# A sparse-attention and RWKV-7 trunk: another order in its weave, other buffers for rotation and compression, one score pass moved ahead

## The chip, the cores and the metric

The kernel runs on one core of one Trainium2 chip. The time is the device time of one execution in microseconds (us). Five engines take part: PE (TensorE, with its weight loads as PEld), DVE (VectorE), ACT (ScalarE), POOL (GpSimd) and SP (SyncE), which here issues all DMAs, one behind the other.

## The reference

One layer on x of 1024 tokens by 1024 channels, then a final RMSNorm. All arithmetic is float32.

```python
h = rms_norm(x, norm_g)
proj = h @ w_in                      # one projection, its columns for two groups of heads
# group B, 8 heads of 64: RWKV-7, a state per head
state = state * w + (state @ -kk) (kk * a) + v k ;  y = state @ r
# y: normed by group, plus a bonus, times silu(g_rwkv)
# group A, 8 heads of 64 on 2 K/V heads: three attentions
k_cmp, v_cmp = compress_blocks(...)  # 32-token blocks: silu(flat @ w1) @ w2
o_cmp = softmax(q k_cmp) v_cmp ;  top 8 blocks of 64 by its probabilities
q_rot, ks, kw = partial_rope(...)    # 16 of 64 dimensions rotated
o_sel = attention over the 8 chosen blocks ;  o_win = over a window of 512
# gated sum of the three, times silu(g_nsa)
x + concat(A, B) @ w_out
```

## The kernel before, in words

**Filler.** The projection runs as a stream of matmuls of 128 by 512, the filler: for each column group three products (high by high, high by low, low by high, of operands that are split in two parts: `gn2h` and `gn2l` are the two parts of `gn2r`, a weight as it is loaded; `gn` are four groups of the gate of group A, `gr` of the gate of group B). `filler.step(n)` puts n of them into PE's order. A group's weights come in two halves; a half is loaded, ACT copies it to the high part (L342), DVE subtracts for the low one (L344).

**Weave.** The recurrence of group B runs over eight chunks of 128 tokens, one weave each (`weave(n)`, L1242). A weave has 12 steps. A step puts a burst of small matmuls of the chain into PE's order (`pc`, `py`; the chain is what hands the state on from chunk to chunk), then half of its filler quota (7 or 8 matmuls in all), then the side pieces of the step, then the other half. Side pieces prepare the next chunks: elementwise work (`pss`, `pt`, `pbt`, `pn`), products (`pp`), a triangular inverse in 31 steps on POOL (`lt`, `ltmp`, L584 and L586, for which `la` is loaded through DRAM: `la<-dA`), values, and the norm of the chunk before (`nq`, `ny`, `pyn`). From the table in the program each side piece has its step.

**Seam.** In weaves 6 and 7 the buffers of the elementwise work have become free and a pool for group A is opened, with six buffers under the one tag c4. `rotate()` (L755) turns q and the window and selection keys: it loads q and keys twice (`ropa`, and `ropw` with the two halves exchanged), and tables of cosines and sines (`ropc`, `rops`); DVE multiplies `ropa` (L777), POOL `ropw` (L778), DVE adds (L781), ACT copies the sum to its high part `roph`, POOL subtracts for the low one `ropl` (L785), and four stores per set go out. `compress(b)` (L793) loads keys or values (`kc`), their weights w1 in four tiles and w2; DVE and POOL add positions (`xc`, L815), PE multiplies (`pcm`, 16 matmuls for each of the four w1 tiles).

**Prologue.** After the last weave come 12 filler matmuls, the norm of chunk 7, and then, under an order by hand for PE, the first score passes of group A: `row_max` finds the maximum score of each row (PE writes scores to `pd` and `ps`, DVE reduces them to `bm`, L982 and L994), PE turns the result (`pnm`), DVE writes it into q (L1009). `compressed` does the attention over compressed blocks (`pcs`, `pct`, `poc`). Between the pieces stand filler matmuls.

**Stages.** Then follow eight query tiles in the order (1, 5, 4, 3, 6, 2, 7, 0), each in two branches b=0 (chosen blocks) and b=1 (window). A branch computes scores `pst`, exponentials `prob` (ACT), their sums `acc` (POOL) and values `po`, and at its end `pz`, `prt` (which needs POOL's `wide`). Score passes of the next tile are spread over each branch. POOL also multiplies `yr` by the gate `sg` and splits the output weights (`wol`).

**Order.** PE's and POOL's order in the weaves, and PE's alone behind them, is that of the program text. The order of DVE, ACT and SP is set by a scheduler from priorities and its own simulated times. Each engine runs its list strictly in order.

Of the kernel before, what the change touches and what calls it, by code (L numbers as in the profile page):

```python
# [20 lines left out]
S = 1024  # L21
# [53 lines left out]
def trunk_kernel(ctx, tc, x, norm_g, w_in, cmp_pos_k, cmp_w1_k, cmp_w2_k, cmp_pos_v, cmp_w1_v,  # L75
# [666 lines left out]
    def split_out(scale, dfull, dh, dl, rows0):  # L742
# [9 lines left out]
            dma(dl[rows0:rows0 + 128, hs], al)  # L752
        return use

    def rotate():  # L755


        ct, sn = c4([128, S], FT, "ropc"), c4([128, S], FT, "rops")
        sets = []
        for src, dh, dl in ((dQ, dQH, dQL), (dKFa, dKHa, dKLa)):  # L760
            v = src.rearrange("(h d) t -> h d t", d=64)
            n = v.shape[0] * 8
            a, w = c4([128, S], FT, "ropa"), c4([128, S], FT, "ropw")
            if n < 64:
                for t in (a, w):
                    G.memset(t[n:64], 0.0)
            for hf in range(2):
                rows = slice(hf * 64, hf * 64 + n)
                dma(a[rows], v[:, hf * 8:hf * 8 + 8, :])
                dma(w[rows], v[:, 8 - hf * 8:16 - hf * 8, :])  # L770
            sets.append((slice(0, 64 + n), n, a, w, dh, dl))
        for i, tb in enumerate((ct, sn)):
            for hf in range(2):
                dma(tb[hf * 64:hf * 64 + 64], rope[i:i + 1, hf * 8:hf * 8 + 8].to_broadcast([8, 8, S]))
        yield
        for rows, n, a, w, dh, dl in sets:
            V.tensor_tensor(a[rows], a[rows], ct[rows], op=OP.mult)  # L777
            G.tensor_tensor(w[rows], w[rows], sn[rows], op=OP.mult)  # L778
            yield
        for rows, n, a, w, dh, dl in sets:  # L780
            V.tensor_tensor(a[rows], a[rows], w[rows], op=OP.add)  # L781
            h_ = c4([128, S], FR, "roph")
            A.activation(h_[rows], a[rows], AF.Copy)
            l_ = c4([128, S], FR, "ropl")
            G.tensor_tensor(l_[rows], a[rows], h_[rows].bitcast(FT), op=OP.subtract)  # L785
            for d, t in ((dh, h_), (dl, l_)):
                v = d.rearrange("(h d) t -> h d t", d=64)
                for hf in range(2):
                    dma(v[:, hf * 8:hf * 8 + 8, :], t[hf * 64:hf * 64 + n])
            yield  # L790


    def compress(b, w1, w2):  # L793
# [9 lines left out]
        s2 = cp.tile([128, 2, 126], FT, tag="cs2", name="cs2", bufs=1)  # L803

        def load(q):
            wt = c4([128, 4, 256], FT, "w1")
            dma(wt, w1v[:, q * 4:q * 4 + 4, :])
            return wt

# [435 lines left out]
    def weave(n, sides, quota):  # L1245


        chain = wkv_chain(n)
        for j in range(12):
            with tc.high_priority(offset=200000):  # L1250
                next(chain)
            filler.step(quota // 2)
            for gen in sides.get(j, ()):
                piece(gen)
            filler.step(quota - quota // 2)
        whole(chain)

    TRI, EDGE, TRI_T, EDGE_T = range(4)
# [6 lines left out]
    def c4(shape, dt, name):  # L1265
        return cp.tile(shape, dt, tag="c4", name=name, bufs=6)
# [36 lines left out]
    with tc.manual_schedule(engines={E.PE, E.Pool}):  # L1303
        keys = []
        nxt_elem = wkv_load(2) or wkv_elementwise(2)

        def call(f):
            f()
            yield

        for n in range(8):
            sides = {}

            def side(gen, *steps):
                for j in steps:
                    sides.setdefault(j, []).append(gen)

            elem = nxt_elem
            if n < 7:
                side(wkv_values(n + 1), 0, 1)  # L1320
                inv = wkv_inverse(n + 1)
            if n < 6:
                side(elem, *((0, 1, 2, 3, 3, 4, 5, 8) if n == 0 else (0, 1, 2, 3, 4, 5, 8)))
            if 0 < n < 7:
                side(prod, 0, 1, 2, 3, 4, 5)
            if n > 0:
                side(wkv_norm(n - 1), 0, 2, 4)
            if n < 6:
                prod = wkv_products(n + 2)
                side(prod, 6, 7, 7, 10, 11)  # L1330
            if n < 5:
                def ahead(n=n):
                    if n == 1:
                        filler.through("v3")
                    wkv_load(n + 3)
                nxt_elem = wkv_elementwise(n + 3)
                side(call(ahead), 2)
                side(nxt_elem, 11)
            if n < 7:
                side(inv, 9, 10, 11)  # L1340
            if n == 6:
                side(call(open_keys), 1)

                def begin(gen):
                    keys.append(gen)
                    next(gen)

                def nxt(k, *steps):
                    for j in steps:
                        side(call(lambda: next(keys[k])), j)  # L1350

                side(call(lambda: (filler.through("q3"), begin(rotate()))), 1)
                nxt(0, 6, 7, 8, 9)
                side(call(lambda: begin(compress(0, cmp_w1_k, cmp_w2_k))), 9)
            if n == 7:
                nxt(1, 0, 1, 2, 3, 4, 5)
                side(call(lambda: begin(compress(1, cmp_w1_v, cmp_w2_v))), 3)
                nxt(2, 6, 7, 8, 9, 10, 11)
            weave(n, sides, (7, 7, 7, 8, 8, 8, 7, 7)[n])
        for g in keys:  # L1360
            assert next(g, None) is None
        norm = wkv_norm(7)
        next(norm)
        next(norm)
        filler.step(12)
        next(norm)
# [30 lines left out]
    with tc.manual_schedule(engines=PEQ):  # L1397
        L = load_queries(TILES[0], 0)
        dma(keep, late[:, L_IMP:])
        load_keys(0)  # L1400
        load_keys(1)
        L1 = load_queries(TILES[1], 1)
        load_values(0)
        load_values(1)
        comp, rm0, rm1 = compressed(TILES[0], L), row_max(TILES[0], 0, L), row_max(TILES[0], 1, L)
        com1 = compressed(TILES[1], L1)
        filler.step(30)
        for gen, n in ((comp, 10), (rm0, 5), (rm0, 5), (comp, 5), (rm0, 5), (rm0, 5), (comp, 5),
                       (rm1, 5), (com1, 5), (rm1, 5), (rm1, 5), (rm1, 5), (rm0, 8), (com1, 5),
                       (rm1, 5), (com1, 0)):  # L1410
            next(gen)
            filler.step(n)
        for gen in (comp, rm0, rm1, com1):
            assert next(gen, None) is None
        filler.through("gr3")
# [56 lines left out]
    with tc.manual_schedule(engines=PEQ):  # L1472
        for n, i in enumerate(TILES):
# [7 lines left out]
            for b in range(2):  # L1481
# [4 lines left out]
                if b == 0:  # L1486
                    if n:
                        side.add(row_max(i, 1, L), row_max_pieces(i, 1), 0.0, 0.8)
                    if 0 < n < 7:
                        side.add(compressed(j, L1), 3, 0.0, 0.9)  # L1490
                elif n < 7:
                    side.add(row_max(j, 0, L1), row_max_pieces(j, 0), 0.0, 0.8)
                if n == 1:
                    side.add(wout, 4)
# [44 lines left out]
```

## Time and profile before

| what | value |
|---|---|
| three runs | 1043.26 us median (1038.44 to 1045.9) |
| the profiled execution | 1040.26 us, span 1038.5 us |
| PE busy | 930.2 us, 90% of the span, 6353 matmuls |
| DVE, ACT, POOL busy | 584.0, 335.5, 448.2 us |
| granted clock of PE, mean | 0.951 |
| the chain that ended last | PE 60%, DVE 10%, DMA 9%, POOL 7%, SP's issue 6% |

Busy time is what instructions took on an engine; the rest of the span the engine waited or had nothing. The chain is followed back from the last instruction to what released each one. In the trace, weaves 0 to 5 run from 198 to about 480 us, weave 6 from 480.8, weave 7 from 527.6 to about 583; the prologue begins at 594, the stage of the first tile at 650, that of the second at about 676.

### The profile page before, as it was taken

How to read it: one execution, taken by the hardware profiler on the slowest of the kernel's cores; microseconds unless marked ns; L12 is line 12 of the kernel's file. 1: busy time of each engine (PE TensorE's matmuls, PEld its weight loads, DVE VectorE, ACT ScalarE, POOL GpSimd, SP SyncE). 2: the span in 40 equal slices, each digit the busy share in tenths (PEclk: the TensorE clock that was granted, in tenths of full speed). 3: DMA queues.
4: the chain of work that ended last, by engine and by line, in shares of the span. 5: the costliest groups of instructions: out<-in, count | busy, mean ns of one | idle time of the engine just before them, and what ended most of it. 6: DMA issues, size and time to landing. Idle time of an engine off the chain costs nothing.

```text
span 1038.5 us, 17087 instructions
## 1 busy us (share of the span) xinstructions
PE 930.2 (90%) x6353; PEld 658.6 (63%) x6353; DVE 584.0 (56%) x1245; ACT 335.5 (32%) x650; POOL 448.2 (43%) x732
## 2 busy tenths in 40 slices
PE   5999999989998999899669978689999999889976
PEld 4888777766676766677458756354565656455555
DVE  7533545555575657374424335677659856685544
ACT  5533233224233443243121212433333333224321
POOL 3100153466483847444521120577463555246521
PEclk9999999999999999799889988879999999899989
DMA  7433453424426453536476293741132312231121
GB/s 259 125 102 102 125 157 108 130 76 116 135 76 172 134 154 119 131 106 170 116 218 192 65 203 95 212 122 31 41 63 79 77 46 69 53 80 33 39 84 41
DMA packets 154429, 115.66 MB, mean 111 GB/s; under 512 B 54369, under 2 KB 132266, under 8 KB 154346
## 3 DMA queue, kind: packets, MB, share of 16 engines
q1 hardware_dynamic: 154346, 114.57, 40.3%
q8 instruction: 50, 0.82, 0.3%
q14 instruction: 33, 0.27, 0.1%
HBM read 76.19 MB, written 35.19 MB: 107 GB/s over the span
## 4 chain that ended last, share of the span: by engine, by line
PE 60%; DVE 10%; DMA 9%; POOL 7%; SPq 6%; issue 5%; ACT 2%; POOLq 0%; DVEq 0%; ACTq 0%
PE pout L113 7%; SPq L85 6%; PE pst L113 6%; PE po L113 5%; PE p_r L113 4%; PE p_k L113 3%; PE p_gn L113 3%; PE p_gr L113 3%; PE p_q L113 3%; PE pc L113 2%; POOL lt L586 2%; POOL ltmp L584 2%; PE ps L113 2%; PE pd L113 2%; PE pcm L113 2%
## 5 line engine op out<-in xcount | busy, mean ns | idle before, releaser
L584 POOL TENSOR_TENSOR ltmp<-la,lt 128x60 f32<-128x60 f32 (+24 forms) x248 | 83.7, 337 | 65.3 <-DMA la<-dA 42.7
L1042 ACT ACTIVATE prob<-pst 128x512 f32<-128x512 f32 x132 | 74.6, 593 | 109.9 <-PE pst L113 106.3
L1055 POOL TENSOR_TENSOR acc<-acc,prob 128x1024 f32<-128x1024 f32 x36 | 86.7, 2409 | 45.1 <-ACT prob L1042 44.9
L586 POOL TENSOR_TENSOR lt<-lt,ltmp 128x60 f32<-128x60 f32 (+24 forms) x248 | 87.6, 353 | 18.8
L113 PE MATMUL pst<-q,k 128*128 128x512 f32 (+1 forms) x264 | 82.3, 430 | 0.0
L994 DVE TENSOR_REDUCE bm<-ps 128x6 f32<-128x384 f32 (+1 forms) x106 | 63.5, 613 | 26.6 <-PE ps L113 26.0
L113 PE MATMUL po<-prob,vt 128*64 128x512 f32 x264 | 75.1, 648 | 0.0
L1055 POOL TENSOR_TENSOR acc<-prob 128x1024 f32<-128x1024 f32 x14 | 33.7, 2410 | 82.6 <-ACT prob L1042 82.6
L113 PEld LDWEIGHTS pst<-q,k 128*128 128x128 f32 (+1 forms) x264 | 48.9, 196 | 14.9 <-issue 5.7
L113 PE MATMUL pout<-woh,mh 128*128 128x512 f32 x128 | 57.6, 450 | 0.2 <-DVE xt L1153 0.2
L113 PE MATMUL ps<-k,q 128*128 128x384 f32 (+3 forms) x136 | 45.4, 386 | 7.7 <-DVE bm L994 3.7
L113 PE MATMUL pout<-wol,mh 128*128 128x512 f32 x128 | 51.3, 401 | 0.0
L113 PE MATMUL pout<-woh,ml 128*128 128x512 f32 x128 | 51.2, 400 | 0.0
L113 PEld LDWEIGHTS ps<-k,q 128*128 128x128 f32 x136 | 25.6, 205 | 35.2 <-DVE bm L994 14.3
L982 DVE TENSOR_REDUCE bm<-pd 128x8 f32<-128x512 f32 x40 | 27.4, 688 | 26.2 <-PE pd L113 26.0
L113 PEld LDWEIGHTS pout<-woh,mh 128*128 128x128 f32 x128 | 25.1, 196 | 20.7 <-issue 17.8
L683 ACT ACTIVATE x<-pc 64x128 f32<-64x128 f32 x32 | 8.7, 272 | 75.4 <-DVE x L682 75.2
L113 PE MATMUL pd<-k,q 128*128 128x128 f32 x160 | 31.1, 321 | 2.1 <-POOL k L868 2.1
L1077 POOL TENSOR_TENSOR wide<-rr,ones 128x512 f32<-128x512 f32 x16 | 17.1, 1068 | 36.1 <-DVE rr L1073 34.1
L1069 DVE TENSOR_REDUCE zz<-pz 128x4 f32<-128x512 f32 x32 | 21.8, 684 | 13.4 <-PE pz L1067 13.0
L1153 DVE TENSOR_TENSOR xt<-pout,xt 128x512 f32<-128x512 f32 x16 | 11.1, 691 | 32.4 <-PE pout L113 32.4
L113 PEld LDWEIGHTS pd<-k,q 128*128 128x128 f32 x160 | 25.9, 204 | 4.0 <-POOL k L868 2.4
(518 smaller groups left out, 2447.7 us busy)
## 6 DMA issues: line engine op xcount, KB each, us to landing
dM<-mix SPq DMA_DIRECT2D x24, 256.0 KB
q<-dQH SPq DMA_DIRECT2D x22, 256.0 KB
la<-dA SPq DMA_DIRECT2D x32, 128.0 KB
xt<-in_x_dram SPq DMA_DIRECT2D x8, 512.0 KB
out_dram<-xt SPq DMA_DIRECT2D x16, 256.0 KB
x<-in_x_dram SPq DMA_DIRECT2D x7, 512.0 KB
mixk<-dM SPq DMA_DIRECT2D x8, 256.0 KB
mixr<-dM SPq DMA_DIRECT2D x8, 256.0 KB
```

Source lines behind the costliest of these rows:

```text
L85: return nc.sync.dma_start(plain(o), plain(i))
L113: return T.matmul(o, l, r, start=start, stop=stop)
L584: G.tensor_tensor(tv, la[:, j:j + 1, j + 1:].to_broadcast([128, m, n]), lt[:, :m, j:j + 1].to_broadcast([128, m, n]), op=OP.mult)
L586: G.tensor_tensor(lt[:, :m, j + 1:], lt[:, :m, j + 1:], tv, op=OP.add)
L683: gate["A"] = A.activation(x1[1][HP[1], c:8:4, :], pv[HP[1], :, 64:128], AF.Copy)
L982: V.tensor_reduce(bm[:, g * 4:g * 4 + 4, j:j + 2], p.rearrange("p (r b c) -> p r b c", b=2, c=64), axis=AX.X, op=OP.max)
L994: V.tensor_reduce(bm[:, h0:h0 + n, j:j + 2 * w], p[:, :n * w * 128].rearrange("p (h b c) -> p h b c", h=n, c=64), axis=AX.X, op=OP.max)
L1042: A.activation(pr[:, g * 512:(g + 1) * 512], p, AF.Exp)
L1055: G.tensor_tensor(s, self.acc, pr, op=OP.add)
L1069: V.tensor_reduce(zz[:, g, :], p.rearrange("p (r k) -> p r k", r=4), axis=AX.X, op=OP.add)
L1077: G.tensor_tensor(wide, rr.rearrange("p r g -> p (r g)").unsqueeze(2).to_broadcast([128, 8, 64]), ones64.unsqueeze(1).to_broadcast([128, 8 ...
L1153: V.tensor_tensor(xt[:, hs], p, xt[:, hs], op=OP.add)
```

## The change

It has four parts. (a) In a weave the side pieces of a step stand directly behind the burst, and the whole filler quota follows them. (b) The tables of `rotate` lie in two buffers that the RWKV part no longer uses (tags g0, g1), and its split is made in place: ACT copies the sum into `ropw`, POOL subtracts in `ropa`; the four w1 tiles of the first `compress` lie in four such buffers (ar, la, g0, g1). (c) In weave 6 the steps of `rotate` are 7 to 10, where they were 6 to 9; the first `compress` is begun at step 6 and runs at steps 9, 10, 11 of weave 6 and 0, 1, 2 of weave 7, where it was begun at 9 and ran at 0 to 5 of weave 7; the second is begun at step 0 and runs at 4 to 9, where it was 3 and 6 to 11. (d) The score pass of the second tile for b=0 moves from the first stage (its branch b=1) to the end of the prologue, with three filler matmuls behind each of its pieces; the prologue begins with 40 filler matmuls where it had 30, and has fewer between its pieces.

```diff
@@ -752,10 +752,16 @@
             dma(dl[rows0:rows0 + 128, hs], al)
         return use
 
+    def spare(tag):
+
+        if tag == "la":
+            return r2("la", 1, (128, 32, 32)).rearrange("p a b -> p (a b)")
+        return r2(tag, 3, (128, 8, 2, 64)).rearrange("p a b c -> p (a b c)")
+
     def rotate():
 
 
-        ct, sn = c4([128, S], FT, "ropc"), c4([128, S], FT, "rops")
+        ct, sn = (spare(t) for t in ("g0", "g1"))
         sets = []
         for src, dh, dl in ((dQ, dQH, dQL), (dKFa, dKHa, dKLa)):
             v = src.rearrange("(h d) t -> h d t", d=64)
@@ -779,11 +785,9 @@
             yield
         for rows, n, a, w, dh, dl in sets:
             V.tensor_tensor(a[rows], a[rows], w[rows], op=OP.add)
-            h_ = c4([128, S], FR, "roph")
-            A.activation(h_[rows], a[rows], AF.Copy)
-            l_ = c4([128, S], FR, "ropl")
-            G.tensor_tensor(l_[rows], a[rows], h_[rows].bitcast(FT), op=OP.subtract)
-            for d, t in ((dh, h_), (dl, l_)):
+            A.activation(w.bitcast(FR)[rows], a[rows], AF.Copy)
+            G.tensor_tensor(a.bitcast(FR)[rows], a[rows], w[rows], op=OP.subtract)
+            for d, t in ((dh, w.bitcast(FR)), (dl, a.bitcast(FR))):
                 v = d.rearrange("(h d) t -> h d t", d=64)
                 for hf in range(2):
                     dma(v[:, hf * 8:hf * 8 + 8, :], t[hf * 64:hf * 64 + n])
@@ -803,7 +807,8 @@
         s2 = cp.tile([128, 2, 126], FT, tag="cs2", name="cs2", bufs=1)
 
         def load(q):
-            wt = c4([128, 4, 256], FT, "w1")
+            wt = c4([128, 4, 256], FT, "w1") if b else (
+                spare(("ar", "la", "g0", "g1")[q]).rearrange("p (u c) -> p u c", c=256))
             dma(wt, w1v[:, q * 4:q * 4 + 4, :])
             return wt
 
@@ -1249,10 +1254,9 @@
         for j in range(12):
             with tc.high_priority(offset=200000):
                 next(chain)
-            filler.step(quota // 2)
             for gen in sides.get(j, ()):
                 piece(gen)
-            filler.step(quota - quota // 2)
+            filler.step(quota)
         whole(chain)
 
     TRI, EDGE, TRI_T, EDGE_T = range(4)
@@ -1350,12 +1354,13 @@
                         side(call(lambda: next(keys[k])), j)
 
                 side(call(lambda: (filler.through("q3"), begin(rotate()))), 1)
-                nxt(0, 6, 7, 8, 9)
-                side(call(lambda: begin(compress(0, cmp_w1_k, cmp_w2_k))), 9)
+                nxt(0, 7, 8, 9, 10)
+                side(call(lambda: begin(compress(0, cmp_w1_k, cmp_w2_k))), 6)
+                nxt(1, 9, 10, 11)
             if n == 7:
-                nxt(1, 0, 1, 2, 3, 4, 5)
-                side(call(lambda: begin(compress(1, cmp_w1_v, cmp_w2_v))), 3)
-                nxt(2, 6, 7, 8, 9, 10, 11)
+                nxt(1, 0, 1, 2)
+                side(call(lambda: begin(compress(1, cmp_w1_v, cmp_w2_v))), 0)
+                nxt(2, 4, 5, 6, 7, 8, 9)
             weave(n, sides, (7, 7, 7, 8, 8, 8, 7, 7)[n])
         for g in keys:
             assert next(g, None) is None
@@ -1404,12 +1409,15 @@
         load_values(1)
         comp, rm0, rm1 = compressed(TILES[0], L), row_max(TILES[0], 0, L), row_max(TILES[0], 1, L)
         com1 = compressed(TILES[1], L1)
-        filler.step(30)
-        for gen, n in ((comp, 10), (rm0, 5), (rm0, 5), (comp, 5), (rm0, 5), (rm0, 5), (comp, 5),
-                       (rm1, 5), (com1, 5), (rm1, 5), (rm1, 5), (rm1, 5), (rm0, 8), (com1, 5),
-                       (rm1, 5), (com1, 0)):
+        rm2 = row_max(TILES[1], 0, L1)
+        filler.step(40)
+        for gen, n in ((comp, 8), (rm0, 4), (rm0, 4), (comp, 4), (rm0, 3), (rm0, 3), (comp, 3),
+                       (rm1, 3), (com1, 3), (rm1, 3), (rm1, 3), (rm1, 3), (rm0, 4), (com1, 3),
+                       (rm1, 3), (com1, 3)):
             next(gen)
             filler.step(n)
+        for _ in rm2:
+            filler.step(3)
         for gen in (comp, rm0, rm1, com1):
             assert next(gen, None) is None
         filler.through("gr3")
@@ -1488,7 +1496,7 @@
                         side.add(row_max(i, 1, L), row_max_pieces(i, 1), 0.0, 0.8)
                     if 0 < n < 7:
                         side.add(compressed(j, L1), 3, 0.0, 0.9)
-                elif n < 7:
+                elif 0 < n < 7:
                     side.add(row_max(j, 0, L1), row_max_pieces(j, 0), 0.0, 0.8)
                 if n == 1:
                     side.add(wout, 4)
```

PE in weave 3: the last product of a burst (`py`), the side pieces of that step (`pss`, `pt`) and filler (`p_kw`). Before:

```order
L113 MATMUL py<-g_2337,x_2593 64x64
L113 MATMUL p_kw<-hh_109,kwh 128x512
L113 MATMUL p_kw<-hh_109,kwl 128x512
L113 MATMUL p_kw<-hl_111,kwh 128x512
L113 MATMUL pss<-mi,s_3703 128x2 x4
L113 MATMUL pt_3713<-tt,t_3612 32x32 x16
L113 MATMUL p_kw<-hh_109,kwh 128x512
L113 MATMUL p_kw<-hh_109,kwl 128x512
L113 MATMUL p_kw<-hl_111,kwh 128x512
L113 MATMUL p_kw<-hh_109,kwh 128x512
```

The same place now:

```order
L113 MATMUL py<-g_2334,x_2590 64x64
L113 MATMUL pss<-mi,s_3700 128x2 x4
L113 MATMUL pt_3710<-tt,t_3605 32x32 x16
L113 MATMUL p_kw<-hh_109,kwh 128x512
L113 MATMUL p_kw<-hh_109,kwl 128x512
L113 MATMUL p_kw<-hl_111,kwh 128x512
L113 MATMUL p_kw<-hh_109,kwh 128x512
L113 MATMUL p_kw<-hh_109,kwl 128x512
L113 MATMUL p_kw<-hl_111,kwh 128x512
L113 MATMUL p_kw<-hh_109,kwh 128x512
```

Three filler matmuls that stood ahead of the side pieces stand behind them.

SP in weave 6, behind the loads for `rotate` of q and of the keys (`dKFa`). Before:

```order
L85 DMA ropa<-dKFa 32x1x1024
L85 DMA ropw<-dKFa 32x1x1024
L85 DMA ropc<-in_rope_dram 64x1x1024 x2
L85 DMA rops<-in_rope_dram 64x1x1024 x2
L85 DMA nq<-dS_101 128x512
L85 DMA w_5937<-in_cmp_w_k_dram 128x2x64
L85 DMA gn2r<-in_w_in_dram 128x4x64 x2
L85 DMA dSG<-silu 128x512 x2
L85 DMA dY<-ny 128x2x256
```

The same place now (the tables are loaded earlier there, into `g_5644` and `g_5645`, and a tile of w1, `ar<-in_cmp_w_k_dram`, earlier still):

```order
L85 DMA ropa<-dKFa 32x1x1024
L85 DMA ropw<-dKFa 32x1x1024
L85 DMA kc_5839<-dKC_92 64x1024
L85 DMA kc_5839<-dKC_92 64x1023
L85 DMA kc_5842<-dKC_92 64x1024
L85 DMA nq<-dS_101 128x512
L85 DMA kc_5842<-dKC_92 64x1023
L85 DMA w_5845<-in_cmp_w_k_dram 128x2x64
L85 DMA gn2r<-in_w_in_dram 128x4x64 x2
L85 DMA dSG<-silu 128x512 x2
L85 DMA dY<-ny 128x2x256
L85 DMA la<-in_cmp_w_k_dram 128x4x256
```

The four loads of the tables have left this place, and four of `kc` have come, three of them ahead of `nq` and all ahead of `gn2r`.

DVE in weave 6, from the second half of the norm (`ny`) to the first additions of `rotate`. Before:

```order
L726 SCALAR_TENSOR_TENSOR ny<-ny,cols,nq 128x256 x2
L669 COPY z<-pc 128x128
L777 TENSOR_TENSOR ropa<-ropa,ropc 128x1024
L344 TENSOR_TENSOR gn2l<-gn2r,gn2h 128x512
L682 COPY x_4969<-pc 64x2x64
L777 TENSOR_TENSOR ropa<-ropa,ropc 96x1024
```

The same place now (L783 is the multiplication that was L777):

```order
L726 SCALAR_TENSOR_TENSOR ny<-ny,cols,nq 128x256 x2
L669 COPY z<-pc 128x128
L344 TENSOR_TENSOR gn2l<-gn2r,gn2h 128x512
L682 COPY x_4965<-pc 64x2x64
L783 TENSOR_TENSOR ropa<-ropa,g_5644 128x1024
L689 COPY x_4965<-pc 64x2x64
```

The low part of the filler's weights, `gn2l`, stands ahead of the multiplication where it stood behind it.

## Rows read from the trace of the kernel before

**Rows 1.** Windows: window, its length, engines' busy time (instructions), clock, DMA share, GB/s.

```profile
198.00:480.00 282.00, 264.86 (x2666) 189.12 (x2665) 164.30 (x395) 99.22 (x216) 164.62 (x415) 0.96 0.44 123
...
594.00:631.00 37.00, 26.26 (x118) 19.56 (x117) 12.96 (x22) 4.17 (x7) 5.79 (x4) 0.84 0.93 190
650.00:676.00 26.00, 16.22 (x68) 8.79 (x67) 18.16 (x23) 10.80 (x16) 14.61 (x9) 0.82 0.74 212
```

**Rows 2.** Waits of PE, 198 to 480 us: releaser, us in total, times, longest.

```profile
PE pss L113 <- ACT s L467: 5.9, 4, 2.1
...
PE pp L113 <- DVE bk L525: 3.0, 4, 1.0
...
PE px L113 <- DVE t L633: 1.4, 3, 0.6
```

**Rows 3.** Timeline, 378 to 407: start, length, engine, instruction, [idle before, releaser].

```profile
378.53 0.24 POOL L584 TENSOR_TENSOR ltmp<-la,lt 128x31 f32<-128x31 f32 x1 [5.28 <-DMA la<-dA]
...
405.65 0.75 DVE L525 TENSOR_TENSOR bk<-s,s 128x512 f32<-128x512 f32 x1 [1.42 <-POOL s L522]
...
406.46 1.16 PE L113 MATMUL pp<-ar,bk 64*128 64x128 f32 x16 [0.76 <-DVE bk L525]
```

**Rows 4.** Timeline of PE in weaves 6 and 7.

```profile
500.45 0.40 PE L113 MATMUL p_gn<-hh,gn2h 128*128 128x512 f32 x1
500.68 0.40 PE L113 MATMUL p_gn<-hh,gn2l 128*128 128x512 f32 x1
...
505.41 0.49 PE L113 MATMUL p_gn<-hh,gn2h 128*128 128x512 f32 x1 [4.10 <-ACT gn2h L342]
510.79 0.80 PE L113 MATMUL p_gn<-hh,gn2l 128*128 128x512 f32 x1 [4.89 <-DVE gn2l L344]
...
540.69 3.48 PE L113 MATMUL pcm<-xc,w 128*128 128x126 f32 x16 [8.02 <-DMA w<-in_cmp_w_k_dram]
...
546.45 1.94 PE L113 MATMUL pcm<-xc,w 128*128 128x126 f32 x16
```

**Rows 5.** Timeline of DVE, ACT, SP, POOL around the first stall.

```profile
503.66 0.88 DVE L726 SCALAR_TENSOR_TENSOR ny<-ny,cols,nq 128x256 f32<-128x256 f32 x2 [5.53 <-DMA nq<-dS]
...
504.66 3.34 DVE L777 TENSOR_TENSOR ropa<-ropa,ropc 128x1024 f32<-128x1024 f32 x1
507.92 2.82 DVE L344 TENSOR_TENSOR gn2l<-gn2r,gn2h 128x512 fp32r<-128x512 f32 x1
...
504.72 0.63 ACT L342 ACTIVATE gn2h<-gn2r 128x512 fp32r<-128x512 f32 x1 [6.88 <-DMA gn2r<-in_w_in_dram]
...
495.89 0.33 SPq L85 DMA_DIRECT2D nq<-dS  x1
...
504.57 5.62 POOL L778 TENSOR_TENSOR ropw<-ropw,rops 128x1024 f32<-128x1024 f32 x2
```

**Rows 6.** Windows before and behind the first stall (columns of rows 1).

```profile
492.00:496.00 4.00, 4.00 (x36) 3.13 (x33) 1.55 (x7) 0.27 (x1) 3.53 (x8) 1.00 0.51 202
...
512.00:516.00 4.00, 4.00 (x21) 2.75 (x21) 1.42 (x2) 0.27 (x1) 0.00 (x0) 0.50 0.51 94
```

**Rows 7.** Groups on PE, 650 to 671 us: count, busy, mean ns, idle before them.

```profile
L113 PE MATMUL ps<-k,q 128*128 128x512 f32 (+1 forms) x16 | 4.8, 385 | 1.1 <-DVE bm L994 0.7 <-DVE bm L982 0.2
...
L113 PE MATMUL pd<-k,q 128*128 128x128 f32 x8 | 1.4, 308 | 0.0
...
L1008 PE MATMUL pnm<-ident,nm 128*104 128x128 f32 x1 | 0.5, 456 | 7.8 <-DVE nm L1006 7.8
```

**Rows 8.** Timeline of POOL and PE in the first stage.

```profile
660.04 1.29 POOL L1134 TENSOR_TENSOR yr<-yr,sg 128x512 f32<-128x512 f32 x1 [5.61 <-DMA sg<-dSR]
...
673.78 1.04 POOL L1077 TENSOR_TENSOR wide<-rr,ones 128x512 f32<-128x512 f32 x1 [1.09 <-DVE rr L1073]
674.78 5.12 POOL L1114 TENSOR_TENSOR wol<-wor,woh 128x1024 fp32r<-128x1024 f32 x2
...
674.88 1.12 PE L1081 MATMUL prt<-ident,wide 128*128 128x128 f32 x4 [0.85 <-POOL wide L1077]
```

## The prediction made before the change was timed

> **What bounds the kernel now.** First the windows by stage: in the weaves PE is busy 264.86 of 282 us at a clock of 0.96 [rows 1]. So PE is the bound almost everywhere, and a change pays only where PE stands still or runs at its lower clock. Then PE's own waits say where that is. In weaves 0 to 5 they are small: `pss` 5.9 us in four waits, `pp` 3.0 in four, `px` 1.4 in three [rows 2]. In weaves 6 and 7 they are large: 4.10 and 4.89 us for the two parts of a filler weight, 8.02 us for compression weights [rows 4]. In the first stage PE is busy only 16.22 of 26.0 us [rows 1], and 7.8 of the rest is one wait, `pnm` for a maximum of DVE [rows 7]. Last, the prologue until 631: 26.26 of 37 us busy, with the DMA engines at 0.93 [rows 1], so this stretch is bound by loads.
>
> The sum is made against the profiled execution, 1040.26 us. The median shown, 1043.26, is 3.0 above it, and I add that at the end.
>
> **(a) Side pieces behind the burst: 0.** No work comes or goes. Three or four filler matmuls no longer stand ahead of a side piece. One filler step is 0.23 us (500.45 to 500.68) [rows 4], three are 0.7. So a side piece whose operand is made late waits 0.7 us longer, and the same filler then runs behind it. What may pay this back is a loop that PE does not set: POOL begins the triangular inverse when `la` has landed, at 378.53, and `bk`, for which POOL's L522 must come round behind that inverse, is made at 405.65; then `pp` starts at 406.46 [rows 3]. These 27 us, and the stores and loads from `pp` back to `la` (POOL stood idle 5.28 us for `la` [rows 3]), don't shrink or grow with PE's order. Where PE loses 0.7 at `pss`, it arrives later at `pp` and waits less there. The waits at `pp` are only 0.76 to 1.0 apiece, so the exchange is about even. From below: some pieces start their DVE and ACT work 0.7 us earlier, which may take away the 3.0 us at `pp`. From above: each of four kinds of side pieces that wait now or nearly (`pss`, `pp`, `px` and the norm's) loses 0.7 in seven weaves, 28 x 0.7 = 19.6. I take 0, since `pp`'s row is the nearest to a loop that stays.
>
> **(b, c) The seam: -7.5.** Before, it costs 4.10 + 4.89 + 8.02 = 17.0 us of waiting [rows 4]. The clock falls too: after the first stall it is 0.50 in 512 to 516, all 4.00 us of them busy [rows 6], so about 2.0 us are lost there, and the first `pcm` group takes 3.48 where a later one takes 1.94 [rows 4], 1.5 us. Together 20.5. The edits in turn:
>
> The 8.02 is the wait for a w1 tile that stood behind the stores of the rotated keys. Now these tiles go into buffers that are free long before, the first of them ahead of `rotate`'s loads. With the 1.5 of cold clock it goes: -9.5.
>
> In its place comes a new one: the first `pcm` now belongs to step 10 of weave 6, and POOL's addition for it (`xc`) stands behind both multiplications of `rotate` (5.62 us for two [rows 5]) and one subtraction of it. From below it costs nothing, if the first stall has given POOL the time. From above it is one more operation of POOL of that size and its own DVE and ACT ahead, some 5.62 us. I take 2.5, near the middle, since a stall ahead remains.
>
> The first stall, 9.0 us, has three steps. `nq` is issued at 495.89 and lands only when DVE's wait of 5.53 us ends at 503.66; the weight `gn2r`, issued behind it, releases ACT at 504.72; DVE then does the multiplication of `rotate` (3.34 us) before `gn2l` (2.82), at whose end PE goes on [rows 5]. Now `gn2l` stands ahead of that multiplication: up to -3.3. Against it, three loads of `kc` (256 KB each, 0.79 MB) are new in SP's list between `rotate`'s loads and `nq`, a fourth stands before `gn2r`, and 0.5 MB of w1 stand further ahead. At the 202 GB/s of 492 to 496 [rows 6], 1.05 MB are 5.2 us later for `gn2r`; but the DMA engines were only 0.51 busy then [rows 6], so half of it, 2.6, if new loads use the idle half. I take +2.6, because the busy share is the nearer row: first stall 9.0 - 3.3 + 2.6 = 8.3, with the same 2.0 us of cold clock. From below the stall goes down to 4, from above it is 9.0 - 0 + 5.2 = 14.2.
>
> The Trainium skill, in DMA: Bandwidth & Descriptors, section "Why a DMA increments its semaphore by 16 and not by 1", says that a transfer runs on the largest number of engines up to 16 that divides the slowest dimension on both of its sides. By that the loads of `rotate`, made of 8 heads by 8 rows, use 8 engines and those of `kc`, with 64 rows, 16; the share of 0.51 agrees, and by it the delay would be the 2.6. In the SBUF page (SBUF — State Buffer, section "Who interferes with whom") one rule speaks against the change: of a DVE operation with two SBUF inputs and a GpSimd operation that reads SBUF, the one that begins later waits for the whole of the other. By it `gn2l` would stay as slow beside POOL's multiplication wherever it stands; the 2.82 us of it agree, and no run here shows it alone at that place.
>
> Seam: -9.5 + 2.5 - 0.7 = -7.7, and I take 0.2 off for the in-place split, whose stores read buffers that are then reused: -7.5. Bounds: -20.5 + 4 = -16.5 from below, -9.5 + 5.6 + 5.2 = +1.3 from above.
>
> **(d) First stage and prologue: -2.5.** The moved pass is `ps` 4.8 us, `pd` 1.4 and `pnm` 0.5 on PE [rows 7], with the mask products some 7.5. It comes to the prologue's end, where PE has work for every moment: +7.5. The filler there is the same in number, and what the larger first 40 cover cannot be gained while loads bound the stretch [rows 1]. The stage loses 7.5 of work, 1.1 of waiting at `ps`, and the 7.8 at `pnm` [rows 7]: by PE alone 26.0 [rows 1] would become 9.6. But `prt` needs POOL's `wide`, and POOL's `yr` stands ahead of it, which waited for `sg` until 660.04, 10.0 us into the stage, and takes 1.29; `wide` takes 1.04 [rows 8]. So `prt` can't come before 12.4, where it came at 24.9 [rows 8]. The stage shrinks by 12.5, not by 16.4. Behind it POOL's two weight splits, 5.12 us [rows 8], now lie nearer to the second stage's sums: between 0 and 5.12, I take 2.5. Sum: +7.5 - 12.5 + 2.5 = -2.5. Bounds: if `sg` lands sooner and nothing is passed on, 7.5 - 16.4 = -8.9, and with a clock that no longer falls some 2 more, -11; if POOL passes on all 5.1 and DVE delays `pnm` in the prologue by 3, +3.
>
> **Sum.** 0 - 7.5 - 2.5 = -10.0: 1030.3 beside the profiled 1040.3, **1033** beside the median.
>
> **Rivals.**
> *All waits go (0.22).* `kc` and w1 lie in idle time, `rotate` is done before `pcm` needs it, and the first stage has no new wait: -16.5 - 8.9 = -25, and some of it is given back at `pp`: about 1020. For it: DMA share 0.51 and 0.74 at those places. Against it: `nq` took 7.67 us to land with less in front of it.
> *The waits only change place (0.15).* `gn2r` later by the full 5.2, `pcm` waiting 5.6 for POOL, POOL's lag of 5.1 in the second stage: +1.3 in the seam and about 0 behind it: 1043 to 1046. That the new buffers don't help, since each tile still waits for `rotate`, is in it.
> *Slower: the side pieces lose their cover (0.15).* PE, not POOL, sets the weave's period, and 28 side pieces lose 0.7 each. 19.6 - 10.0 = +9.6: 1053. For it: `pss` waits longest of all now, and for an ACT operation that PE's order doesn't hasten. It decides when PE's idle time in 198 to 480 grows from 17 to over 27 us. Against it: most side pieces have no wait at all now.
> *Forecast (0.48)*: 1026 to 1040.
>
> A difference within 1% (1032.8 to 1053.7) can't be told from none here. Faster by more than that: all of the second case and half of the forecast's, 0.46. Slower: half of the last, 0.09, and some for a stretch that I have not costed, 0.12. The rest, 0.42, is within. The range must reach from the case of no waits to near the slower one: 1016 to 1052.
>
> **What the new profile would show.** (a) PE's waits in 198 to 480 with `pss` near 9 us and `pp` near 0, idle time still about 17. (b, c) No wait of PE for a DMA of w1; `gn2l` on DVE at once after `gn2h`; `nq` landing 2 to 3 us later; `pcm` waiting for `xc` or not at all. (d) `pnm` without a wait in the prologue, the first stage some 13 us long, `prt` waiting for `wide`. The prediction is wrong if the weaves lengthen by more than 3 us, if the first stall grows beyond 10, or if the second stage takes up what the first gives.

## The result, and the profile after

The changed kernel takes 1057.08 us (median of 4 runs, 1054.32 to 1063.89), the kernel before 1042.72 in the same comparison: a ratio of 1.0147, 95% interval 1.0098 to 1.0195. It is slower by 14 to 15 us, and the forecast was 1033. The profiled execution has a span of 1056.4 us, 17.9 more than before. PE does the same work (6353 matmuls, 928.5 us busy), so what was added is waiting.

PE's waits of the whole execution (releaser, us in total, times, longest), the first ones:

```profile
PE p_gn L113 <- ACT gn2h L342: 12.4, 1, 12.4
PE prt L1086 <- POOL wide L1082: 11.6, 4, 4.5
PE pss L113 <- ACT s L467: 10.5, 5, 3.4
...
PE ps L113 <- DVE bm L987: 8.4, 2, 7.9
PE pnm L1013 <- DVE nm L1011: 7.9, 5, 2.6
...
PE pp L113 <- DVE bk L525: 6.3, 4, 3.2
...
PE pcm L113 <- POOL xc L820: 3.9, 1, 3.9
```

Against [rows 2], `pss` has 4.6 us more and `pp` 3.3 more, neither paid for the other. The 8.02 us for w1 [rows 4] are gone, and so is the 7.8 for `pnm` in the first stage [rows 7]. In their place stand 12.4 us for a filler weight and 7.9 at `ps` in the prologue, and `prt` waits 11.6 us for `wide` where it waited 8.0.

Where the time went shows best between landmarks that both traces have: the first `z` copy of DVE that lies in weave 0 and the first in weave 6, the start of the last `pyn` of PE, POOL's first and third `wide`, and the end. All in us, one profiled execution each, with the runs of parts that are told below:

| kernel | to weave 0 | weaves 0 to 5 | weaves 6, 7 | to first `wide` | to third `wide` | rest | span |
|---|---|---|---|---|---|---|---|
| before | 205.2 | 276.1 | 112.6 | 79.9 | 45.3 | 319.4 | 1038.5 |
| changed | 206.9 | 285.1 | 114.9 | 75.9 | 52.2 | 321.3 | 1056.4 |
| (a) alone | 210.1 | 283.9 | 112.2 | 80.9 | 49.8 | 317.9 | 1054.8 |
| (b), (c) alone | 207.4 | 274.9 | 114.3 | 80.1 | 47.7 | 322.2 | 1046.6 |
| (d) alone | 206.1 | 277.1 | 115.7 | 77.4 | 51.6 | 320.4 | 1048.2 |
| (d), old filler | 208.2 | 279.9 | 114.2 | 71.6 | 54.3 | 316.8 | 1044.9 |

The first column, which no part touches, differs by up to 4.9 us from kernel to kernel, so single differences of a few us in this table are no evidence; the ratios below are. The other columns scatter too. Weaves 0 to 5 take 274.9 to 281.5 us in the traces of eight kernels that leave them as before, at mean granted clocks of 0.98 to 0.93; the longest of the eight is the kernel with all parts but (a). From the first to the third `wide`, eight kernels without (d) take 44.8 to 50.6 us, so the 45.3 of the kernel before is near the low end.

**Seam.** The timeline of the changed kernel, weave 6, SP, DVE and PE (start, length, instruction, idle before and its releaser):

```profile
494.93 0.99 SPq L85 DMA_DIRECT2D gn2r<-in_w_in_dram  x2
...
506.44 4.96 SPq L85 DMA_DIRECT2D kc<-dKC  x3
514.23 0.34 SPq L85 DMA_DIRECT2D nq<-dS  x1
516.63 0.44 SPq L85 DMA_DIRECT2D kc<-dKC  x1
...
521.08 1.49 SPq L85 DMA_DIRECT2D gn2r<-in_w_in_dram  x2
...
525.96 0.88 DVE L726 SCALAR_TENSOR_TENSOR ny<-ny,cols,nq 128x256 f32<-128x256 f32 x2 [13.11 <-DMA nq<-dS]
...
528.39 0.69 DVE L344 TENSOR_TENSOR gn2l<-gn2r,gn2h 128x512 fp32r<-128x512 f32 x1 [1.35 <-ACT gn2h L342]
...
528.41 0.79 PE L113 MATMUL p_gn<-hh,gn2h 128*128 128x512 f32 x1 [12.39 <-ACT gn2h L342]
...
544.53 1.82 PE L113 MATMUL pcm<-xc,ar 128*128 128x126 f32 x7 [3.90 <-POOL xc L820]
```

They answer to [rows 4, 5]. `gn2l` follows `gn2h` at once, as forecast; it takes 0.69 us with POOL standing idle, where it took 2.82 beside POOL's multiplication [rows 5], and that gain was in no term. But the second pair of `gn2r` is issued only at 521.08, 6.8 us behind `nq`; before, it was issued at 496.80, 0.9 behind. (The last line ends where the view does; the whole `pcm` group has 16 matmuls.)

**First and second stage**, timeline of POOL, then DVE and PE, the prologue's end:

```profile
681.65 1.26 POOL L1139 TENSOR_TENSOR yr<-yr,sg 128x512 f32<-128x512 f32 x1 [1.03 <-DMA sg<-dSR]
682.87 1.04 POOL L1082 TENSOR_TENSOR wide<-rr,ones 128x512 f32<-128x512 f32 x1
683.99 4.70 POOL L1119 TENSOR_TENSOR wol<-wor,woh 128x1024 fp32r<-128x1024 f32 x2
...
642.33 0.69 DVE L344 TENSOR_TENSOR gr3l<-gr3r,gr3h 128x512 fp32r<-128x512 f32 x1 [8.96 <-ACT gr3h L342]
...
645.60 1.12 PE L113 MATMUL ps<-k,q 128*128 128x128 f32 x4 [7.86 <-DVE bm L987]
...
683.97 0.66 PE L1086 MATMUL prt<-ident,wide 128*128 128x128 f32 x4 [4.52 <-POOL wide L1082]
```

`prt` waits for `wide` behind `yr`, as forecast from [rows 8]. At `ps` PE waits 7.86 us for DVE, which had itself waited 8.96 us for a gate weight (`gr3h`) and came to `bm` behind the low part of it and three other operations.

### The profile page after: what moved, and what is told of

Same layout as the page of the kernel before. It is cut to its first block, busy times and chain, and to the rows that moved or that the text cites. A ratio compares the mean times of both kernels' runs of the same rounds, so it can differ in the third digit from the quotient of the medians.

```text
span 1056.4 us, 17094 instructions
## 1 busy us (share of the span) xinstructions
PE 928.5 (88%) x6353; PEld 666.0 (63%) x6353; DVE 587.6 (56%) x1245; ACT 334.3 (32%) x650; POOL 444.6 (42%) x732
## 4 chain that ended last, share of the span: by engine, by line
PE 62%; DVE 12%; DMA 10%; issue 6%; SPq 4%; POOL 3%; ACT 2%; POOLq 0%; DVEq 0%; ACTq 0%
PE pout L113 6%; PE pst L113 5%; PE po L113 5%; PE p_r L113 4%; SPq L85 4%; PE p_gr L113 3%; PE p_k L113 3%; PE p_v L113 3%; PE pc L113 3%; PE p_q L113 3%; PE p_gn L113 2%; PE ps L113 2%; PE p_kc L113 2%; PE pp L113 2%; PE pcm L113 2%
## 5 line engine op out<-in xcount | busy, mean ns | idle before, releaser
L113 PE MATMUL pst<-q,k 128*128 128x512 f32 (+1 forms) x264 | 84.9, 441 | 1.3 <-ACT prob L1047 1.3
L1060 POOL TENSOR_TENSOR acc<-prob 128x1024 f32<-128x1024 f32 x14 | 33.7, 2411 | 47.3 <-ACT prob L1047 45.3
```

The source lines that it names most:

```text
L113: return T.matmul(o, l, r, start=start, stop=stop)
L1060: G.tensor_tensor(s, self.acc, pr, op=OP.add)
```

## The experiments

Each was timed in five rounds against the kernel before.

**Part (a) alone.** The diff is the piece in `weave` only.

```diff
-            filler.step(quota // 2)
             for gen in sides.get(j, ()):
                 piece(gen)
-            filler.step(quota - quota // 2)
+            filler.step(quota)
```

> The kernel before with part (a) alone: side pieces directly behind the burst. Theory 'cover lost' (in the changed kernel the weaves lost about 7.5 us at pss and pp): weaves 0 to 5 longer by 6 to 9 us, PE's wait at pss in 198 to 490 near 10 us where it was 5.9, whole kernel +7 to +12 us. Rival 'the seam alone': the weaves lose only where the compression loads disturb them, so here within 2 us of before.

Measured: ratio 1.0112 (1.0073 to 1.0151), some 12 us slower: the largest part. The window of weaves 0 to 5 of this kernel (columns of [rows 1]), and behind it PE's waits in it:

```profile
210.10:494.00 283.90, 254.38 (x2595) 191.02 (x2596) 161.87 (x380) 95.11 (x207) 161.50 (x410) 0.93 0.43 119
```

```profile
PE pss L113 <- ACT s L467: 10.5, 5, 3.4
PE pp L113 <- DVE bk L525: 6.5, 5, 2.1
PE pc L113 <- ACT x L690: 4.3, 3, 1.6
```

The rival theory of the seam falls by the ratio, since no load of the seam has moved here. The weaves are 7.8 us longer than before, at a mean clock of 0.93 for 0.96 [rows 1], and 285.1 in the changed kernel; both lie above the 281.5 that the kernels without (a) reach, but the size is no exact one. Two waits set these two kernels apart from all eight that leave these weaves as before: `pss`, 10.5 us in five waits where the eight have 5.2 to 7.2 in four, and `pc` for L690, 3.1 and 4.3 against at most 0.4. The 6.5 at `pp` do not, since the eight read 2.9 to 6.6. What `pss` waits for is told by ACT's timeline of this kernel around one of its waits, and PE's; the last line is PE at the same place in the kernel before:

```profile
291.33 0.60 ACT L697 ACTIVATE nq<-py 128x512 f32<-128x512 f32 x1 [1.62 <-PE py L113]
291.95 0.27 ACT L690 ACTIVATE x<-pc 64x128 f32<-64x128 f32 x1
292.25 0.84 ACT L699 ACTIVATE ny<-py,cols 128x256 f32<-128x256 f32 x2
292.98 0.90 ACT L467 ACTIVATE s<-mixk,cols 128x256 f32<-128x256 f32 x2
...
293.53 1.45 PE L113 MATMUL pss<-mi,s 128*128 128x2 f32 x8 [2.25 <-ACT s L467]
...
284.44 1.05 PE L113 MATMUL pss<-mi,s 128*128 128x2 f32 x8 [1.36 <-ACT s L467]
```

The operand of `pss` needs nothing of the burst. But ACT, in order, makes it behind operations that do need the burst of the same step: a square and two scaled copies of `py`, and a copy of `pc`. So the 2.6 us of ACT's work, `s` included, begin when the burst ends, and the filler between burst and `pss` was all the cover there was: 1.36 us of waiting with three filler matmuls ahead, 2.25 with none.

**Parts (b) and (c) alone** (the diff of the change without its pieces in `weave` and behind line 1400).

> The kernel before with parts (b) and (c) alone: other buffers for the rotation and the compression, and their pieces at other steps. Theory 'SP's list': gn2r is issued behind the rotation's and the compression's loads, PE waits 8 to 13 us for gn2h, the wait for w1 is gone; sum between -3 and +5 us. Rival 'the seam is only late because (a) was': the first stall is about 8 us and the 8.0 us for w1 are gone, so -6 to -9 us.

Measured: 1.0009 (0.9982 to 1.0036), no difference. PE's two waits at the seam:

```profile
517.60 0.80 PE L113 MATMUL p_gn<-hh,gn2h 128*128 128x512 f32 x1 [15.27 <-ACT gn2h L342]
...
534.09 3.15 PE L113 MATMUL pcm<-xc,ar 128*128 128x126 f32 x15 [3.06 <-POOL xc L820]
```

(The view ends inside the last group, which has 16 matmuls and takes 3.36 us.) The waits were 4.10 + 4.89 + 8.02 [rows 4] and are 15.27 + 3.06: 1.3 us more. So the wait for w1 was exchanged for a later `gn2r`, whether (a) is there or not, and the second theory falls. The first was right on the exchange, and the stall was 2.3 us above the range that it gave. What held `gn2r` back is first of all on SP. Its own waits from the first load of `ropa` to the issue of `gn2r`, in 486 to 512 of this kernel, first, and in 482 to 498 of the kernel before, are:

```profile
SPq L85 <- DMA g<-in_rope_dram: 4.1, 3, 1.5
SPq L85 <- DMA ropw<-dQ: 4.0, 2, 2.5
SPq L85 <- DMA ropa<-dQ: 3.2, 2, 1.8
SPq L85 <- DMA ropa<-dKFa: 2.9, 2, 1.6
SPq L85 <- DMA ropw<-dKFa: 2.3, 2, 2.0
```

```profile
SPq L85 <- PE pyn L720: 2.6, 1, 2.6
SPq L85 <- DMA ropa<-dQ: 1.0, 1, 1.0
SPq L85 <- DMA ropw<-dQ: 0.9, 1, 0.9
```

SP, which issues in the order of its list, waits 16.5 us (the sum of the first five rows) for earlier loads to land, where it waited 1.9 (the last two). By the kernel's text none of the loads that it waits for goes into a buffer of `kc`, of `w` (the weights w2) or of `gn2r`, whose loads stand behind them. Every load behind them in the list is late too: here `gn2r` is issued at 511.07, 16 us after the last load of `rotate` (495.02).

**Part (d) alone** (the diff of the change behind line 1400).

> The kernel before with part (d) alone: score pass of the second tile in the prologue. Theory 'the work behind it is squeezed': first stage 3 to 5 us shorter over prologue and stage together, second stage (b=0 and b=1 of the second tile) 8 to 11 us longer, sum +4 to +8 us. Rival 'the second stage only suffered from what lay before': second stage unchanged, sum -3 to -5 us.

Measured: 1.0057 (1.0028 to 1.0087), 6 us slower: the sum of the first theory. Its two parts came out smaller than it said, 2.5 us shorter to the first `wide` and 6.3 longer behind it, and only the first is clear of the scatter: eight traces without (d) take 79.7 to 81.8 us up to there, the three with (d) as it was 75.9 to 77.4. From the first to the third `wide` the kernels with (d) take 48.7 (all but (a)) to 54.3 us, 51.7 in the mean of four, and the eight without it 48.2 in the mean of 44.8 to 50.6. So some 3.5 us there may be (d)'s, and most of its 6 us is not placed by the traces.

**All but (a).**

> The changed kernel without part (a). If the parts add up: its time is that of the changed kernel less what part (a) alone costs, so 1045 to 1050 us. Rival 'the parts act on each other' (the late weave moves the loads of the seam): below 1040 us.

Measured: 1.0065 (1.0038 to 1.0092). The parts add up by their ratios: 1.0009 and 1.0057 give 1.0066, and with (a) 1.0178, within the interval of the whole change (1.0098 to 1.0195).

**The squares of `pss` one step earlier, in the kernel before.** A `yield` behind the two ACT operations of L467, and one step more for the piece (and one piece more ahead of the first weave and in it, left out here).

```diff
             A.activation(sq[:, FI[fi]], k[:, FI[fi]], AF.Square, scale=kkc(2 * fp + fi))
+        yield
         p = psE("pss")
...
-                side(nxt_elem, 11)
+                side(nxt_elem, 10, 11)
```

> The kernel before, with the two ACT squares that pss needs (L467) put into the step before pss, everything else as before. Theory 'pss waits for an ACT operation that stands behind the copies of its own step's burst': pss's waits (5.9 us in four) go, and the lower clock behind them too: 4 to 9 us faster than before. Rival 'POOL's loop sets the weave': the waits move to pp, whole kernel within 2 us.

Measured: 1.0014 (0.9981 to 1.0047), the rival's value. PE's waits in 205 to 481 us begin with

```profile
PE pp L113 <- DVE bk L526: 6.7, 5, 2.6
PE pc L113 <- ACT x L684: 2.6, 2, 1.7
PE px L113 <- DVE t L634: 1.6, 3, 0.7
```

`pss` no longer waits at all, and `pp` waits 6.7 us where it waited 3.0. In four of these five waits DVE's `bk` had itself waited for POOL. So it looks as if the loop over POOL gave back 3.7 of the 5.9 us, but kernels without this change read up to 6.6 at `pp`; that it sets the period is not shown.

**The same with part (a).**

> Part (a) with the squares one step earlier. If (a) costs 12 us because the pieces behind the burst have lost their cover, and pss is the largest of them, most of it is gone: within 4 us of before. Rival 'the chain's own ACT copies are hindered by side pieces that come earlier' (PE waits at pc for L690 and L683): still 8 us or more over before.

Measured: 1.0028 (0.9999 to 1.0058), where (a) alone gave 1.0112. About 9 of its 12 us are gone (the two intervals leave 4 to 14), so the cover of `pss` was most of what (a) cost. The rival has a share: in 207 to 491 us, PE waits 5.9 us at `pc` for L691 (before: 0.2 for that line), behind 9.9 at `pp`. PE's idle time by itself is not the price: it is 25.8 us in weaves 0 to 5 here and 16.8 before, and they take 276.5 us here and 276.1 before.

**(b) and (c), with the loads of `kc` behind `gn2r`.** The four loads got a dependency on the second half of `gn2r`.

> Parts (b) and (c), with the four loads of kc kept back until the second half of gn2r has landed. Theory 'SP's list': the first stall (15.3 us in the run with (b) and (c) alone) falls below 8 us since gn2r is issued ahead of kc; pcm may wait 3 to 6 us for xc; sum 5 to 9 us faster than before. Rival 'the tables and w1 alone fill the DMA engines': gn2r lands as late, the stall stays over 12 us, no gain over (b) and (c) alone.

Measured: 1.0011 (0.9976 to 1.0047), no gain; the rival holds. PE's first stall is still 12.6 us, now at a `pc` whose ACT copy stands behind `gn2h`. SP issues `gn2r` at 504 and 507, behind the tables and the loads of the rotation, and it lands in their wake. Counted from the first `z` of weave 6, its second load is issued 9.2 us earlier than with (b) and (c) alone (at 20.3, there 29.5), but ACT can begin on it only 5.0 earlier (at 29.6, there 34.6; before, 23.4). So the issue is not all that made `gn2r` late; the way from issue to landing grew from 5.1 us to 9.2.

**Buffers of (b), the rotation's loads behind `nq`.** The loads of `ropa`, `ropw` and `kc` depend on that of `nq`; rotation is begun at step 5, compression at 8.

> Buffers of (b); the loads of the rotation's operands and of kc are kept back until nq has landed, and rotation and compression are begun at steps 5 and 8. Theory 'the rotation's loads ahead of nq and gn2r make the first stall': nq and gn2r land before PE wants them, the first stall falls from 9 (before) or 15 (with (b) and (c) alone) to below 3 us, no wait for w1 remains, but the rotation comes later: DVE or POOL may be waited for by 2 to 6 us; sum 6 to 14 us faster than before. Rival 'the loads are too many for the seam wherever they stand': the stall moves to the rotation's operands or to pcm, sum within 4 us of before.

Measured: 0.9990 (0.9957 to 1.0022), again nothing. The waits for the two parts of `gn2` and for w1 are gone, as the theory says, but the rest of it falls. DVE and PE of this kernel:

```profile
511.70 1.23 DVE L783 TENSOR_TENSOR ropa<-ropa,g 128x1024 f32<-128x1024 f32 x1 [6.74 <-DMA ropa<-dQ]
512.84 0.27 DVE L689 COPY x<-pc 64x128 f32<-64x128 f32 x1
...
513.47 0.69 PE L113 MATMUL pc<-x,g 128*64 128x64 f32 x8 [4.58 <-ACT x L690]
...
522.44 0.31 PE L113 MATMUL px<-t,cr 32*32 32x32 f32 x2 [2.87 <-DVE t L633]
525.80 1.05 PE L113 MATMUL px<-t,cr 32*32 32x32 f32 x30 [3.05 <-DVE t L633]
```

The multiplication of `rotate` waits for its load, and the chain's own copy stands behind it on DVE. A fourth wait, 4.35 us, stands ahead of a later `pcm` (546.21); the profile names no releaser, but DVE's `xc` for it ended at 546.11, behind the split of the next filler weight, `gn3`, for which DVE had waited 8.44 us. The orders of the same loads have given stalls of about the same sum: 17.0 us before, 18.3 with (b) and (c) alone, 15.2 with `kc` late and 15.9 here.

**That kernel with the squares earlier.**

> The run before this one with the two squares of pss a step earlier too. The squares alone gave no difference that could be measured (interval -0.2 to +0.5%), so the same as that run within 4 us; if both effects count, up to 6 us below it.

Measured: 0.9931 (0.9898 to 0.9963), 7 us faster than before, and the only version with all of its work done that beats both kernels. The two steps give nothing that can be measured by themselves; that they do together rests on this one interval.

**No weight splits on POOL, without and with (d).** POOL's subtraction for the output weights is left out; ACT copies the weight instead, so that their low parts are not what the reference needs.

```diff
-            G.tensor_tensor(l_, raw, h_.bitcast(FT), op=OP.subtract)
+            A.activation(l_, raw, AF.Copy)
```

> The kernel before with POOL's subtraction for the output weights (L1114, eight of 2.3 us) replaced by a copy on ACT, so the low parts of these weights are not what the reference needs. It is the base for the next run. If POOL paces the first and second stage: 3 to 8 us faster than before; if DVE does: within 3 us.

> Part (d) alone with the same replacement. Theory '(d) costs because the weight splits that ran in the first stage beside DVE's score pass now fall into the second and meet its sums on POOL': against the run before this one no slower, 0 to 6 us faster. Rival '(d) costs in the prologue and on DVE': 5 us or more slower than the run before this one, as with the splits on POOL.

Measured: 0.9945 (0.9913 to 0.9978) and 0.9972 (0.9942 to 1.0002). Taking 20 us of work off POOL (eight splits) is worth 6 us, so POOL counts here. (d) came out 2.8 us slower on top, between what the two theories said. That is 0.27%, where it cost 0.57%: half, but the intervals of the two pairs are each some 0.3% wide to either side, so half can't be told from all or from nothing. Whether the splits are part of what (d) pays stays open.

**(d) with the old filler.**

```diff
+        rm2 = row_max(TILES[1], 0, L1)
         filler.step(30)
...
+        for _ in rm2:
+            filler.step(3)
         for gen in (comp, rm0, rm1, com1):
...
-                elif n < 7:
+                elif 0 < n < 7:
                     side.add(row_max(j, 0, L1), row_max_pieces(j, 0), 0.0, 0.8)
```

> Part (d) alone, but with the prologue's filler as it was: 30 matmuls first, 10 and 5 between the pieces, and three behind each piece of the moved pass. Theory 'the thinner filler lets PE run into loads and DVE' (in the run with (d) alone PE waited 8.8 us at ps for a DVE that was held by the last gate weight, where it was 3.0 before): that wait is 3 to 5 us again and the kernel 3 to 6 us faster than with (d) alone, so within 3 us of before. Rival 'the second stage takes it': the prologue's end and the first stage gain, the stretch behind it is as long as with (d) alone (51 us), and the whole is 4 to 8 us over before.

Measured: 1.0010 (0.9978 to 1.0043), about 5 us better than (d) as it was. So the move by itself costs nothing that can be measured, and most of what (d) costs goes with the thinner filler; the intervals of the two overlap a little, so the 5 us are no exact size. PE waits 5.2 us at `ps`, where with (d) alone it was 8.8. From the last `pyn` to the last filler matmul it is 60.4 us, where it is 66.6 with (d) alone, 65.5 in the changed kernel and 55.6 before: here the thinner filler lost its 5 to 6 us. In the table 8.3 us are won up to the first `wide`, and 9.0 are lost up to the third, of which some 3 lie in the low 45.3 of the kernel before. The time is what the first theory said; of the second, only the long stretch behind came true.

## Why the prediction was wrong

**(a), taken as 0, is where it failed; it costs 12 us.** The step said: where PE loses 0.7 us at `pss`, it waits less at `pp`. The price per piece was about right (0.9 us more per wait at `pss`, 0.7 taken); the payment at `pp` was not. It was to fall to near 0 and reads 6.5 us, which is within what kernels without (a) read, so nothing was paid back that can be seen; `pp` is a side piece behind the burst too, but that it lost cover of its own is argued and was not tried alone. And beside these waits stand three at `pc` behind ACT, 4.3 us, which I had in no term. The rival of the lost cover, put at 19.6 us and a chance of 0.15, was the right mechanism, and its sign came: PE's idle time in weaves 0 to 5 grew to 28.3 us; only the row that I took for the nearest, the idle time of POOL, was that of another engine. The row that decided is in ACT's timeline: `s` stood there behind operations that wait for the burst.

**(b) and (c), taken as -7.5, came to +1 (-2 to +4).** The end of the wait for w1 was right (8.0 of the 9.5), and so was the new wait at `pcm` (2.5 taken, 3.1 measured). The 1.5 us of cold clock taken with w1 did not come: the first `pcm` group took 3.36 us at a granted clock of 0.57 (534 to 538), before 3.48 at 0.53 (540 to 544), since it stands behind a new wait. The first stall was taken as 8.3, at most 14.2, and measured 15.3. These two misses, 1.5 and 7.0 us, account for the way from -7.5 to +1. The row with a busy share of 0.51 had led me to halve the delay. The new loads did not use an idle half: SP, with these parts alone, issued `gn2r` 16 us after the last load of `rotate`, before only 5 (491.93 to 496.80), and counted from the first `z` of weave 6 the weight came 11.2 us later (at 34.6, before 23.4), where 2.6 was taken. The term counted the bytes ahead of a load; what it lacked is the wait of the issuing engine ahead of that load. The run with `kc` late shows that the wait of the load behind its issue counts too.

**(d), taken as -2.5, came to +6 (+3 to +9).** Up to the first `wide` it was right: 7.5 - 12.5 = -5.0 was forecast, -4.0 came in the changed kernel, by the mechanism that was named: the way to the last filler matmul grew by 9.9 us (7.5 taken), and the one from there to `wide` shrank by 13.8 (12.5 taken). So what failed lies behind it: of the 8.5 us that (d) missed by, 1 lies ahead of the first `wide`. The term there is the lag behind the first stage, taken as 2.5 of 5.12. Against the kernel before it reads 6.3 with (d) alone, 6.9 in the changed kernel and 9.0 with the old filler, but 3.5 by the means, and this stretch differs by 6 us between kernels without (d) (44.8 to 50.6). So how much of the miss it makes stays open, and so does what makes it long; POOL's splits may have a share. The filler hid inside the term that came out right: the 7.5 were taken as work in a prologue with no idle moment, but with the old filler the same way grew by only 4.8, so some 5 us of it were cover that the thinner filler had lost.

The median stood 3.0 us above the profiled execution when I forecast; that was right and changed nothing. Of the signs by which I wanted to know, three came true (the end of the waits for w1 and `pnm`, `gn2l` behind `gn2h`, `prt` behind `wide`), and the time came back at other waits: at `gn2h`, `pcm`, `ps` and `prt`. All three signs of being wrong came too: the weaves lengthened by more than 3 us, the first stall grew beyond 10, and the stretch behind the first stage took more than that had given (6.9 against 4.0, by this one pair of traces).

## What to carry to other kernels

Before filler is moved from in front of an instruction, look where its operand stands in its maker's queue: if it is made behind work that starts with the same burst, that filler was its whole cover, and making the operand a step earlier has to come first. A load that is put earlier is put ahead of others in the one list that issues them; read which ones, and whether the issuing engine will still be free to issue. Filler that is thinned out in one place to thicken another was covering something there: put the old filler back before the move itself is judged.

## What was not expected of the hardware

SP waited 16.5 us in 486 to 512 of the kernel with (b) and (c) alone for loads into other buffers than those of `kc`, `w` and `gn2r` behind them, three `kc` issues taking 4.84 us; in the kernel before it was 1.9 up to the same load. What holds SP in such a wait the runs don't show.

PE's clock may make waits dearer than they are long. In the kernel with (a) alone and in the one before, the windows that begin half a microsecond behind the same wait of `pss` (2.25 and 1.36 us) read

```profile
294.00:298.00 4.00, 4.00 (x43) 3.53 (x43) 1.00 (x3) 0.00 (x0) 3.06 (x12) 0.50 0.41 72
```

```profile
285.00:289.00 4.00, 4.00 (x64) 2.94 (x65) 2.43 (x8) 1.11 (x2) 3.14 (x12) 1.00 0.45 92
```

at the lower level (0.50, 1.2 GHz) behind the longer wait and at the higher (1.00, 2.4 GHz) behind the shorter. It is not a rule of that length: behind another wait of 1.36 us, at 236.87 in the kernel before, 240 to 244 us read 0.58.

The whole runs say the same of (a): nine with it alone were granted 0.937 in the mean, those of the kernel before on the same chip 0.949. By a straight line through these runs of the kernel before, which scatter widely about it, 0.01 less goes with some 4 us more; so, as an estimate, about 5 of the 12 us go with the lower clock. Whether the waits lowered it is not shown, and it is not theirs alone: the kernel with all parts but (a) had 0.93 in weaves 0 to 5, too.
